# Parts and tables of the second block's head, its last modulations, unread matmuls at the router and another ring of weight homes

## The chip, the cores and the metric

One core of a Trainium2 chip. The metric is the device time of one launch in microseconds (us), taken as the median of several runs. The kernel before the change stands at 1537.5 us (3 runs, 1537.04 to 1538.98).

## The reference, cut to what matters

Two transformer blocks run one after the other over 256 tokens of 1024 features. The first has two layers (a linear-recurrence mixer over latent and context tokens, then a window attention), each with a squared-ReLU MLP. The second is where most of the change lies:

```python
mod = jax.nn.silu(c) @ w_ada + b_ada
sh1, sc1, g1, sh2, sc2, g2 = jnp.split(mod, 6, axis=-1)
h = _rms(x, norm1_g) * (1.0 + sc1) + sh1
z = h @ w_in                      # rq, rf, ri, rg, aq, ak, av, iq, ik, iw
rec = _hgrn2(rq, rf, ri, rg, ...)            # gated recurrence, 4 heads
att = _dsa_attention(aq, ak, av, iq, layernorm(ik), iw, rel_bias)
x = x + g1 * (concat(rec, att) @ w_out)
h2 = _rms(x, norm2_g) * (1.0 + sc2) + sh2
x = x + g2 * _hier_moe(h2, ...)   # 16 experts in 4 groups, 2 of one group per token
```

`_dsa_attention` scores every key with a small indexer (`iq`, `ik`, `iw`), keeps the best, and adds a bias that is looked up in `rel_bias` by bucket of distance. All of it is float32.

## The kernel before, in words

**Products.** A float32 operand is cut in two parts that TensorE (PE) takes: `split` copies it into the rounded high part (on ScalarE, ACT, or VectorE, DVE) and subtracts that from the source for the low part (L251, on DVE or GpSimd, POOL). A product is then three matmuls, high by high, low by high, high by low (`mm_t` L344 to L346, `mm3` L319 to L321). `wload` brings 1 MB of a weight into a tile of the ring `wr` over SyncE's DMA queue (SP), and `wsplit` cuts it into two tiles of `wh` and two of `wl`; `lengs` names the engine that makes each of the two low parts. `rsqrt` is an addition on DVE (L238 or L240) and a power on POOL (L241).

**Order.** A scheduler places the instructions on their engines, by priority in the order in which the program writes them; every engine then runs its own list in order. `tc.issue_after` holds instructions behind a named one. In the attention loop and the expert part PE's and SP's lists are as the program writes them.

**Modulations.** `fill` (L398 in `mods_ev`) makes one block of 512 columns of a modulation vector with matmuls on raw weights (`wr<-w_ada`). 24 such blocks are spread over the program. `mods_col` (L463) transposes a finished one. The last three, of the second block, are (2,9), after the second MLP, and (2,10) and (2,11), at steps u = 10 and 11 of the head loop.

**Head of the second block.** After the MLP, `x2_chain(a)` normalises token tile a: a layer norm (L1349, L1350) and a root mean square. `transpose_tok` (L506) turns it, and `affine_split` scales, shifts and splits it into `hB` (casts L248, subtractions L251). The weights of `w_in` are split by `p_split(n)` for 16 steps, and `p_step(n)` multiplies: steps 0 and 1 are pp[0] (L1454), whose first matmuls need `hB` and the weight's parts. The indexer's key `ik` gets a separate product (`kraw`, L319 to L321 on 72 columns) and a layer norm (L1494 to L1499) after its transposes; then stand `p_step(3)`, the transposes of the recurrence's keys (L1510), and a table: `rel_bias` by bucket (a DMA on ACT's queue, one matmul L1528, a copy L1530, a DMA to DRAM). Then PSUM's pools are opened anew, and the head loop runs u = 0 to 11: `h_decay(u)` (first matmuls L1544, tile c), `p_step(4 + u)`, scores and outputs of the recurrence.

**Attention loop.** `d_scores` (L1735, L1737, L1739), `d_exp` on ACT, transposes (L1758), products with the values (L1772), and between them parts of `w_out` and the rest of the recurrence's output.

**Router and experts.** `x3` is transposed and multiplied with the router's weights (`logits_half`, L1880 and L1886); a chain of small DVE operations picks the experts; a product (L1989 to L1993) counts the tokens of each; `one_hot` builds selection matrices, and `gather(p0, p1)` (L2052) multiplies them with the high and low parts of `x3` (`parts_in`, L1902). Expert pairs are gathered as (0,2), (6,8), (2,6). Each of 8 pairs runs W3 and W1 (L2138), W2 (L2164) and a scatter (L2186). Its weights come in 12 transfers of 1 MB, each into a home: a tile of `wx` (x) or of `wr` (r) in one piece, or a tile of `wh` and one of `wl` (h), or two of the ring `t4` (b) in halves. The first 16 homes are listed in HOMES, all others in a ring of 15, HOMES_ON. SP issues the transfers in program order, so one that waits for its home holds all behind it. Tiles of `t4` also hold the split `x3`.

## Time and profile before

| what | value |
|---|---|
| median of 3 runs | 1537.5 us |
| profiled execution: time | 1539.3 us |
| its span | 1537.5 us |
| mean granted PE clock (1.0 is full) | 0.968 |
| PE busy | 1425.8 us (93%) |
| DVE, ACT, POOL busy | 973.6, 548.0, 265.4 us |
| DMA | 332.96 MB, mean 217 GB/s |

PE is busy nearly throughout, so the page's shares say little: what counts is where PE waits, at which clock it runs (a granted clock of 0.5 is 1.2 GHz, 1.0 is 2.4 GHz), and, in the expert part from 1287 us on, whether the weights' DMA stream keeps up. Times in the trace are from the start of the span.

### The profile page before, as it was taken

How to read it: one execution, taken by the hardware profiler on the slowest of the kernel's cores; microseconds unless marked ns; L12 is line 12 of the kernel's file. 1: busy time of each engine (PE TensorE's matmuls, PEld its weight loads, DVE VectorE, ACT ScalarE, POOL GpSimd, SP SyncE). 2: the span in 40 equal slices, each digit the busy share in tenths (PEclk: the TensorE clock that was granted, in tenths of full speed). 3: DMA queues.
4: the chain of work that ended last, by engine and by line, in shares of the span. 5: the costliest groups of instructions: out<-in, count | busy, mean ns of one | idle time of the engine just before them, and what ended most of it. 6: DMA issues, size and time to landing. Idle time of an engine off the chain costs nothing.

```text
span 1537.5 us, 22176 instructions
## 1 busy us (share of the span) xinstructions
PE 1425.8 (93%) x8651; PEld 1076.4 (70%) x8651; DVE 973.6 (63%) x1662; ACT 548.0 (36%) x921; POOL 265.4 (17%) x263
## 2 busy tenths in 40 slices
PE   5999999999999999989989899987898997999996
PEld 3688787798887878869767889976786675532332
DVE  2343797789999887686895775575688346112212
ACT  2342333244323222324573445545553333301001
POOL 0033204100132210221131310012425220000000
PEclk9998999999999999999999999997999798999999
DMA  8740564446779876625613955555334836699996
GB/s 290 268 168 2 192 247 143 164 133 212 256 263 323 278 236 223 211 72 188 170 70 130 339 185 196 192 177 167 117 110 148 288 132 224 246 408 410 411 410 263
DMA packets 189394, 332.96 MB, mean 217 GB/s; under 512 B 12665, under 2 KB 67553, under 8 KB 189282
## 3 DMA queue, kind: packets, MB, share of 16 engines
q1 hardware_dynamic: 175152, 298.77, 55.9%
q0 software_dynamic: 8640, 27.85, 5.0%
q10 hardware_dynamic: 5490, 4.85, 1.1%
q8 instruction: 70, 1.15, 0.3%
q14 instruction: 42, 0.34, 0.1%
HBM read 320.91 MB, written 10.53 MB: 216 GB/s over the span
## 4 chain that ended last, share of the span: by engine, by line
PE 33%; DMA 8%; DVE 6%; issue 3%; POOL 2%; ACT 2%; SPq 0%; DVEq 0%; POOLq 0%; ACTq 0%
PE g L2138 5%; PE g L321 2%; PE g L320 2%; PE g L319 2%; PE x L2164 2%; DMA wh<-w_in 2%; PE g L344 2%; PE g L346 2%; PE g L345 2%; DMA wr<-w_in 2%; PE x L345 2%; DMA wx<-w_in 2%; PE x L346 2%; PE x L344 2%; DMA wr<-mlp_w_in 2%
## 5 line engine op out<-in xcount | busy, mean ns | idle before, releaser
L251 DVE TENSOR_TENSOR wl<-wr,wh 128x1024 fp32r<-128x1024 f32 (+1 forms) x206 | 255.6, 1254 | 65.9 <-ACT wh L244 63.8
L244 ACT ACTIVATE wh<-wr 128x1024 fp32r<-128x1024 f32 (+1 forms) x226 | 228.9, 1027 | 178.9 <-PE g L346 93.0
L344 PE MATMUL g<-wh,h 128*128 128x512 f32 (+1 forms) x624 | 248.6, 401 | 12.5 <-DVE t L1402 5.9
L319 PE MATMUL g<-h,wh 128*128 128x256 f32 (+1 forms) x768 | 249.8, 327 | 3.7 <-DVE t L1031 2.6
L321 PE MATMUL g<-h,wl 128*128 128x256 f32 (+1 forms) x768 | 248.1, 324 | 5.4 <-DVE wl L251 5.3
L320 PE MATMUL g<-h,wh 128*128 128x256 f32 (+1 forms) x768 | 249.4, 325 | 0.2 <-DVE h L251 0.2
L345 PE MATMUL g<-wl,h 128*128 128x512 f32 (+1 forms) x624 | 246.2, 395 | 2.7 <-DVE wl L251 2.7
L346 PE MATMUL g<-wh,h 128*128 128x512 f32 (+1 forms) x624 | 245.6, 395 | 2.0 <-DVE h L1707 2.0
L427 DVE SCALAR_TENSOR_TENSOR t<-wr,cT,t 128x512 f32<-128x512 f32 x231 | 172.0, 780 | 12.3 <-DMA wr<-w_ada_in 5.8
L319 PEld LDWEIGHTS g<-h,wh 128*128 128x128 f32 x768 | 145.9, 190 | 19.3 <-DVE t L1031 3.0
L321 PEld LDWEIGHTS g<-h,wl 128*128 128x128 f32 x768 | 146.1, 190 | 18.4 <-DVE wl L251 6.6
L320 PEld LDWEIGHTS g<-h,wh 128*128 128x128 f32 x768 | 146.2, 190 | 12.2 <-DVE h L251 0.6
L344 PEld LDWEIGHTS g<-wh,h 128*128 128x128 f32 x624 | 119.9, 193 | 42.4 <-issue 9.9
L345 PEld LDWEIGHTS g<-wl,h 128*128 128x128 f32 x624 | 120.2, 193 | 27.0 <-DVE wl L251 3.5
L346 PEld LDWEIGHTS g<-wh,h 128*128 128x128 f32 x624 | 119.8, 192 | 27.4 <-DVE h L1707 3.0
L244 ACT ACTIVATE t<-t 128x512 f32<-128x512 f32 (+7 forms) x83 | 47.3, 591 | 133.2 <-DVE t L2169 73.1
L244 ACT ACTIVATE h<-e 128x512 fp32r<-128x512 f32 (+1 forms) x64 | 33.6, 524 | 142.7 <-DVE e L962 142.7
L251 POOL TENSOR_TENSOR wl<-wr,wh 128x1024 fp32r<-128x1024 f32 x20 | 50.5, 2525 | 193.1 <-ACT wh L244 179.8
L244 ACT ACTIVATE t<-x 128x128 f32<-128x128 f32 (+3 forms) x78 | 30.7, 464 | 147.5 <-PE x L2145 109.9
L244 ACT ACTIVATE e<-g 128x512 f32<-128x512 f32 (+1 forms) x72 | 35.5, 493 | 94.5 <-PE g L321 84.8
L241 POOL TENSOR_TENSOR sm<-sm,mhalf 128x1 f32<-128x1 f32 (+2 forms) x33 | 33.1, 1004 | 149.4 <-DVE sm L238 109.0
L2138 PE MATMUL g<-wr,t 128*32 128x512 f32 (+1 forms) x248 | 51.3, 611 | 4.8 <-DMA wr<-w_in 4.7
(429 smaller groups left out, 2162.5 us busy)
## 6 DMA issues: line engine op xcount, KB each, us to landing
wr<-mlp_w_in SPq DMA_DIRECT2D x64, 1024.0 KB
wr<-w_mod_in SPq DMA_DIRECT2D x40, 1024.0 KB
wr<-w_in SPq DMA_DIRECT2D x32, 1024.0 KB
t<-w_in SPq DMA_DIRECT2D x52, 512.0 KB
wr<-w_ada_in SPq DMA_DIRECT2D x24, 1024.0 KB
wr<-w_in_in SPq DMA_DIRECT2D x16, 1024.0 KB
wx<-w_in SPq DMA_DIRECT2D x14, 1024.0 KB
wh<-w_in SPq DMA_DIRECT2D x24, 512.0 KB
```

The lines of the kernel that those rows point to most:

```text
L241: return po.tensor_tensor(o, o, mhalf[:, :o.shape[1]], op=OP.pow)
L244: return ac.activation(o, i, fn, **k)
L251: (leng or ve).tensor_sub(lo, src, hi.bitcast(F32))
L319: pe.matmul(ps, ah, bh, start=start, stop=False)
L320: pe.matmul(ps, ah, bl, start=False, stop=False)
L321: pe.matmul(ps, al, bh, start=False, stop=stop)
L344: pe.matmul(ps, ah[:, tsl], w[0][:, cs], start=start, stop=False)
L345: pe.matmul(ps, ah[:, tsl], w[1][:, cs], start=False, stop=False)
L346: pe.matmul(ps, al[:, tsl], w[0][:, cs], start=False, stop=stop)
L427: ve.scalar_tensor_tensor(s_, S["v"][:, k % 4], c_, s_, op0=OP.mult, op1=OP.add)
L2138: pe.matmul(ps[c:c + n, :], xg[p][k][:, c:c + n], w[a][k], start=k == 0, stop=k == 7, skip_group_check=True, tile_position=(0, c))
L2164: pe.matmul(yp[hf][c:c + n, :], hT_[:, m * 128 + c:m * 128 + c + n], w[a][hf][m], start=m == 0, stop=m == 3, skip_group_check=True, tile_p ...
```

## The change

Seven edits, with no arithmetic added to the result:

1. The bias table moves from behind `p_step(3)` into the second MLP (chunk c = 4).
2. Block (2,9) of the modulations is held behind the last DVE operation of `x2_chain(0)`, and its transpose comes after the split of `kraw`.
3. The splits of n = 1 and 2 of `w_in` are held behind the last operation of `transpose_tok` of token tile 0 and 1, and their low parts go to DVE.
4. In pp[0] the order of the three kinds of matmul becomes high by high, low by high, high by low (the low weights last).
5. `p_step(2)` and `p_step(3)` come before the product of `ik` and before its transposes and layer norm.
6. Blocks (2,10) and (2,11) move from the head loop into the first two turns of the attention loop.
7. `keep_on` puts 4, 12 and 8 matmuls (128x128 by 128x512, bf16), whose results nothing reads, behind the last transposes of `x3`, behind the logits and behind the count; HOMES_ON becomes another ring.

```diff
-        (leng or ve).tensor_sub(lo, src, hi.bitcast(F32))
+        return (leng or ve).tensor_sub(lo, src, hi.bitcast(F32))
...
+        if c == 4:
+
+            rb = t1()[:32, :8]
+            ac.dma_start(rb, I["rel_bias_2"])
+            cload_into(t2(), ["buck"])
+            ps = mmps((8, 384))
+            pe.matmul(ps, rb, CT["buck"][:32], start=True, stop=True)
+            tb = t2()[:8, :384]
+            ve.tensor_copy(tb, ps)
+            btab = dp.tile([8, 384], F32, name="btab")
+            po.dma_start(btab, tb)
...
     hB = Opnd(256)
-    x2_chain(0)
-    fill(len(fills) - NF[4], last=True)
-    ve.scalar_tensor_tensor(sB2, vec(2, 4, 0), 1.0, ncol[:, 8:16], op0=OP.add, op1=OP.mult)
-    transpose_tok(xs[0], hB, 0, sB1, bB1)
+    done = x2_chain(0)
+    with tc.issue_after(done.ins):
+        fill(len(fills) - NF[4])
+    hdone = [transpose_tok(xs[0], hB, 0, sB1, bB1)]
     x2_chain(1)
...
-            pw[n] = wsplit(wload(src), lengs=(po, po) if n == 1 else (ve, po))
+            raw = wload(src)
+            if n < 3:
+                late((hdone[n - 1],), lambda: pw.__setitem__(n, wsplit(raw)))
+            else:
+                pw[n] = wsplit(raw, lengs=(ve, po))
...
-        for a, b in ((0, 0), (0, 1), (1, 0)):
+        for a, b in ((0, 0), (1, 0), (0, 1)):
...
     split(kraw_, ikh, ikl)
+    mods_col(*turns.pop())
+    ve.scalar_tensor_tensor(sB2, vec(2, 4, 0), 1.0, ncol[:, 8:16], op0=OP.add, op1=OP.mult)
+    p_step(2)
     ps = xps((72, 256))
...
-    p_step(2)
+    p_step(3)
     ikT = t1()
...
         later.append(turn)
-    p_step(3)
...
-    for f in later:
-        f()
-    later.clear()
-
-
-    rb = t1()[:32, :8]
-    ac.dma_start(rb, I["rel_bias_2"])
-    cload_into(t2(), ["buck"])
     cload_into(t1(), ["anti"])
-    ps = xps((8, 384))
-    pe.matmul(ps, rb, CT["buck"][:32], start=True, stop=True)
-    tb = t2()[:8, :384]
-    ve.tensor_copy(tb, ps)
-    btab = dp.tile([8, 384], F32, name="btab")
-    po.dma_start(btab, tb)
...
         p_step(4 + u)
-        if u >= 10:
-            fill(last=u == 11)
...
-    HOMES, HOMES_ON = "xxbbrrrrrbbbhhhh", "xxbrrrrrbhhhhbb"
+    HOMES, HOMES_ON = "xxbbrrrrrbbbhhhh", "xxbrrrrrhhhhbbb"
...
             d_scores(i + 1)
+        if i < 2:
+            fill()
...
+        if keep:
+            keep_on(keep, a)
...
+    def keep_on(n, after=None):
 
         with ExitStack() as es:
-            for i_ in after:
-                es.enter_context(tc.issue_after(i_.ins))
-            fn()
+            if after is not None:
+                es.enter_context(tc.issue_after(after.ins))
+            ps = mmps()
+            for _ in range(n):
+                a = pe.matmul(ps.rearrange("p (a b) -> p a b", a=4), ltb, onesb[:, None, :].to_broadcast([128, 4, 128]),
+                              start=True, stop=True, skip_group_check=True)
+        return a
...
-        logits_half(0, cb)
+        aftl = logits_half(0, cb, 4 * cb)
+    keep_on(12, aftl)
...
-        pe.matmul(ps[:, 2], onesb, sel[:, t], start=False, stop=t == 1, skip_group_check=True)
+        aftl = pe.matmul(ps[:, 2], onesb, sel[:, t], start=False, stop=t == 1, skip_group_check=True)
+    keep_on(8, aftl)
```

(`late` itself only moves up, unchanged; the other functions gained a return value.)

How the order moves, at three places.

POOL's list in the second block's head, before: `wl` are low parts of weights, `sm` the powers of the norms, `t` the gate's product in `ev_rf`.

```order
L251 TENSOR_TENSOR wl_9363<-wr_9360,wh_9362 128x1024
L241 TENSOR_TENSOR sm_9243<-sm_9243,mhalf 128x1
L251 TENSOR_TENSOR wl_9367<-wr_9360,wh_9366 128x1024
L241 TENSOR_TENSOR sm_9255<-sm_9255,mhalf 128x1
L251 TENSOR_TENSOR wl_9451<-wr_9444,wh_9450 128x1024
L241 TENSOR_TENSOR sm_9334<-sm_9334,mhalf 128x1
L241 TENSOR_TENSOR sm_9346<-sm_9346,mhalf 128x1
L1373 TENSOR_TENSOR t_1612_9461<-t_1612_9461,t_1374_8073 128x512
L1373 TENSOR_TENSOR t_1614_9467<-t_1614_9467,t_1374_8073 128x512
L251 TENSOR_TENSOR wl_9526<-wr_9519,wh_9525 128x1024
L251 TENSOR_TENSOR wl_9619<-wr_9612,wh_9618 128x1024
L241 TENSOR_TENSOR sm_9591<-sm_9591,mhalf 128x1
```

The same stretch after the change:

```order
L241 TENSOR_TENSOR sm_9253<-sm_9253,mhalf 128x1
L241 TENSOR_TENSOR sm_9265<-sm_9265,mhalf 128x1
L241 TENSOR_TENSOR sm_9340<-sm_9340,mhalf 128x1
L241 TENSOR_TENSOR sm_9352<-sm_9352,mhalf 128x1
L1393 TENSOR_TENSOR t_1615_9467<-t_1615_9467,t_1374_8073 128x512
L1393 TENSOR_TENSOR t_1617_9473<-t_1617_9473,t_1374_8073 128x512
L251 TENSOR_TENSOR wl_9509<-wr_9502,wh_9508 128x1024
L251 TENSOR_TENSOR wl_9602<-wr_9595,wh_9601 128x1024
L251 TENSOR_TENSOR wl_9738<-wr_9731,wh_9737 128x1024
L241 TENSOR_TENSOR sm_9667<-sm_9667,mhalf 128x1
```

The four powers of the two token tiles are no longer mixed with three subtractions; the powers of `ik`'s layer norm (the last row, and one more like it) now have three subtractions ahead of them, where two stood before.

PE's list at the end of the head loop and the start of the attention loop, before (`g<-wr,cT` is a block of modulations, L344 to L346 the last `p_step`, L1735 to L1739 scores; the first of the two blocks stands further up, this is the second):

```order
L344 MATMUL g_10542<-wh_10537,h_1563_9236 128x512
L345 MATMUL g_10542<-wl_10538,h_1563_9236 128x512
L346 MATMUL g_10542<-wh_10537,h_1565_9238 128x512
L398 MATMUL g_10653<-wr_10654,cT_105 32x128 x16
L398 MATMUL g_10653<-wr_10672,cT_105 32x128 x16
L1735 MATMUL s_10722<-t_1591_9357,t_1590_9356 128x256
L1737 MATMUL s_10722<-t_1855_10521,t_1666_9710 128x256
```

After the change, from the same matmul of `p_step` on:

```order
L346 MATMUL g_10542<-wh_10537,h_1569_9248 128x512
L1745 MATMUL s_10644<-t_1594_9363,t_1593_9362 128x256
L1747 MATMUL s_10644<-t_1855_10521,t_1666_9710 128x256
L1749 LDWEIGHTS identb
L1749 MATMUL s_10644<-mb_10458,identb 128x256
L1745 MATMUL s_10648<-t_1594_9363,t_1593_9362 128x256
L1747 MATMUL s_10648<-t_1855_10521,t_1666_9710 128x256
L1749 LDWEIGHTS identb
L1749 MATMUL s_10648<-mb_10458,identb 128x256
L398 MATMUL g_10663<-wr_10664,cT_105 32x128
```

The first score of the attention loop follows the last `p_step` at once. Of the first block one matmul stands behind the second score tile (the last row); the rest of it follows the fourth of the 16 score tiles, and the second block the sixth.

SP's list of weight transfers at W2 of the second pair, before:

```order
L1671 DMA t_2091_11717<-w_2_in 128x1024
L1671 DMA t_2092_11718<-w_2_in 128x1024
L1671 DMA wh_11721<-w_2_in 128x1024
L1671 DMA wl_11722<-w_2_in 128x1024
L1671 DMA wh_11725<-w_2_in 128x1024
L1671 DMA wl_11726<-w_2_in 128x1024
```

After the change:

```order
L1681 DMA wh_11744<-w_2_in 128x1024
L1681 DMA wl_11745<-w_2_in 128x1024
L1681 DMA wh_11748<-w_2_in 128x1024
L1681 DMA wl_11749<-w_2_in 128x1024
L1681 DMA wh_11752<-w_2_in 128x1024
L1681 DMA wl_11753<-w_2_in 128x1024
L1681 DMA wh_11756<-w_2_in 128x1024
L1681 DMA wl_11757<-w_2_in 128x1024
L1681 ISA
L1681 DMA t_2103_11765<-w_2_in 128x2x512
L1681 ISA
L1681 DMA t_2104_11766<-w_2_in 128x2x512
```

Four homes of `wh` and `wl` now stand ahead of the pair of `t4` tiles that stood ahead of them.

## Rows read from the trace of the kernel before

**Rows 1.** The chain that ended last, expert part: start us, us, engine, tile.

```profile
1387.29 12.74 DMA wx<-w_in
```

**Rows 2.** Timeline of SP's queue at W2 of the second pair: start us, us.

```profile
1320.72 15.82 SPq L1671 DMA_DIRECT2D t<-w_in  x2
```

**Rows 3.** Windows: us, busy PE, PEld, DVE, ACT, POOL, PE clock, DMA share, GB/s.

```profile
950.00:1028.00 78.00, 78.00 (x481) 70.42 (x480) 48.38 (x60) 39.32 (x54) 0.00 (x0) 1.00 0.62 202
1212.00:1224.00 12.00, 12.00 (x34) 7.60 (x33) 5.06 (x15) 3.48 (x11) 4.13 (x3) 0.50 1.02 389
1278.00:1280.00 2.00, 1.33 (x8) 1.22 (x8) 1.27 (x4) 1.00 (x1) 0.00 (x0) 0.67 1.07 413
1320.00:1340.00 20.00, 20.00 (x94) 11.39 (x92) 5.48 (x10) 8.11 (x11) 0.00 (x0) 1.00 0.35 126
1380.00:1520.00 140.00, 124.89 (x712) 42.37 (x706) 27.95 (x49) 13.08 (x25) 0.00 (x0) 0.99 1.04 411
```

**Rows 4.** Timeline of POOL in the second block's head: start us, us, engine, line.

```profile
1028.38 3.47 POOL L251 TENSOR_TENSOR wl<-wr,wh 128x1024 fp32r<-128x1024 f32 x1 [112.78 <-ACT wh L244]
1031.82 0.56 POOL L241 TENSOR_TENSOR sm<-sm,mhalf 128x1 f32<-128x1 f32 x1
1032.36 2.34 POOL L251 TENSOR_TENSOR wl<-wr,wh 128x1024 fp32r<-128x1024 f32 x1
```

**Rows 5.** Timeline of DVE, same stretch.

```profile
1028.25 0.15 DVE L238 TENSOR_SCALAR sm<-sm 128x1 f32<-128x1 f32 x1
1028.32 1.28 DVE L1349 SCALAR_TENSOR_TENSOR t<-t,sm,t 128x1024 f32<-128x1024 f32 x1
1032.41 3.37 DVE L1350 SCALAR_TENSOR_TENSOR t<-t,sm,t 128x1024 f32<-128x1024 f32 x1 [2.81 <-POOL sm L241]
```

**Rows 6.** Timeline of PE, same stretch.

```profile
1038.36 1.33 PE L506 MATMUL x<-c_ident,t 128*128 128x128 f32 x5 [4.99 <-DVE t L1352]
...
1043.05 2.07 PE L1454 MATMUL g<-h,h 128*128 128x512 f32 x4 [0.63 <-DVE h L248]
```

**Rows 7.** Timeline of PE behind step 3 of the projections.

```profile
1081.27 1.03 PE L1510 MATMUL x<-c_ident,t 128*128 128x128 f32 x8
...
1086.19 0.80 PE L1528 MATMUL x<-t,t 32*8 32x384 f32 x2 [3.34 <-DMA t<-rel_bias_in]
1087.72 0.77 PE L1544 MATMUL c<-h,t 128*128 128x512 f32 x1 [0.73 <-DVE t L1530]
```

**Rows 8.** Timelines of ACT and DVE, same stretch.

```profile
1081.41 1.06 ACT L244 ACTIVATE wh<-wr 128x1024 fp32r<-128x1024 f32 x1 [0.44 <-PE g L320]
...
1081.29 1.11 DVE L1499 TENSOR_SCALAR t<-x,sm 128x64 f32<-128x64 f32 x4 [2.33 <-POOL sm L241]
```

**Rows 9.** Timeline of PE at the start of the attention loop.

```profile
1197.58 1.96 PE L398 MATMUL g<-wr,cT 128*32 128x128 f32 x64
...
1203.95 0.67 PE L1735 MATMUL s<-t,t 64*128 64x256 f32 x2 [0.50 <-DVE md L400]
...
1210.32 1.17 PE L1735 MATMUL s<-t,t 64*128 64x256 f32 x2 [2.01 <-ACT t L244]
```

**Rows 10.** Timeline of PE at the router and in the first pairs.

```profile
1278.02 1.33 PE L1886 MATMUL o<-t,t 128*128 128x20 f32 x8 [0.80 <-ACT t L244]
1283.88 0.21 PE L1989 MATMUL x<-t 128*128 128x32 bf16 x1 [4.53 <-DVE t L1983]
...
1286.95 6.44 PE L2052 MATMUL x<-h,h 128*128 128x256 f32 x32 [2.80 <-DVE h L2019]
...
1307.89 4.10 PE L2052 MATMUL x<-h,h 128*128 128x256 f32 x32
...
1325.66 1.89 PE L2138 MATMUL g<-wl,t 128*64 128x512 f32 x8
...
1329.42 7.42 PE L2052 MATMUL x<-h,h 128*128 128x512 f32 x32
```

**Rows 11.** Timeline of DVE at the router.

```profile
1277.51 1.28 DVE L1902 SCALAR_TENSOR_TENSOR h<-t,rr,h 128x1024 fp32r<-128x1024 f32 x1 [0.52 <-ACT h L244]
```

More of the change, by code (lines that the diff above doesn't have):

```diff
@@ L489, in affine_split @@
         hi, lo = dst.span(k, nk, c0, c0 + n)
-        split(hv, hi, lo, heng=ve)
+        return split(hv, hi, lo, heng=ve)
     def transpose_in(srcs, dst, c0, sc, bi, ks=range(0, 8, 2)):
@@ L506, in transpose_tok @@
                 pe.transpose(ps[:, j], src[:, c128(k + j)], ident)
-            affine_split(ps, dst, k, 4, c0, 128, sc, bi)
+            a = affine_split(ps, dst, k, 4, c0, 128, sc, bi)
+        return a
     W = I["ev_w_in"][0]
@@ L1328, in emit, with late @@
                 mm_t(accp[t, hf], hids[7], c128(t), k, pw[hf][k], False, k == 3)
+    def late(after, fn):
+        with ExitStack() as es:
+            for i_ in after:
+                es.enter_context(tc.issue_after(i_.ins))
+            fn()
     xs = []
@@ L1351, in x2_chain @@
         ss = rms_rows(zz, w_ if a else xsq)
-        ve.tensor_scalar(w_[:, HF[0]], zz[:, HF[0]], ss, None, op0=OP.mult)
+        done = ve.tensor_scalar(w_[:, HF[0]], zz[:, HF[0]], ss, None, op0=OP.mult)
         act(w_[:, HF[1]], zz[:, HF[1]], AF.Copy, scale=ss)
         xs.append(w_)
+        return done
     hB = Opnd(256)
-    x2_chain(0)
-    fill(len(fills) - NF[4], last=True)
-    ve.scalar_tensor_tensor(sB2, vec(2, 4, 0), 1.0, ncol[:, 8:16], op0=OP.add, op1=OP.mult)
-    transpose_tok(xs[0], hB, 0, sB1, bB1)
+    done = x2_chain(0)
+    with tc.issue_after(done.ins):
+        fill(len(fills) - NF[4])
+    hdone = [transpose_tok(xs[0], hB, 0, sB1, bB1)]
     x2_chain(1)
@@ L1450, in emit @@
         if t:
-            transpose_tok(xs[1], hB, 128, sB1, bB1)
-        for a, b in ((0, 0), (0, 1), (1, 0)):
+            hdone.append(transpose_tok(xs[1], hB, 128, sB1, bB1))
+        for a, b in ((0, 0), (1, 0), (0, 1)):
             for k in range(8):
-                pe.matmul(pp[0][t], hB[k][a][:, c128(t)], pw[k // 4][k % 4][b], start=k + a + b == 0, stop=k + a == 8)
+                pe.matmul(pp[0][t], hB[k][a][:, c128(t)], pw[k // 4][k % 4][b], start=k + a + b == 0, stop=k + b == 8)
     p_split(2)
@@ L1873, in x3_add, with logits_half @@
         return ve.tensor_add(x3[t][:, cs], x3[t][:, cs], tmp)
-    def logits_half(t, cb):
+    def logits_half(t, cb, keep=0):
         ps = pst("s", (128, 4, 128))
         for j in range(4):
-            pe.transpose(ps[:, j], x3[t][:, c128(4 * cb + j)], ident)
+            a = pe.transpose(ps[:, j], x3[t][:, c128(4 * cb + j)], ident)
+        if keep:
+            keep_on(keep, a)
         xT = t2(F32, (128, 4, 128))
@@ L1885, in logits_half @@
         for j in range(4):
-            pe.matmul(lps[t], xT[:, j], wgs[:, 4 * cb + j], start=cb + j == 0, stop=cb + j == 4)
+            a = pe.matmul(lps[t], xT[:, j], wgs[:, 4 * cb + j], start=cb + j == 0, stop=cb + j == 4)
+        return a
     def rms_in(t):
@@ L1903, in parts_in @@
         return a
-    def late(after, fn):
+    def keep_on(n, after=None):
         with ExitStack() as es:
-            for i_ in after:
-                es.enter_context(tc.issue_after(i_.ins))
-            fn()
+            if after is not None:
[4 more added lines that the diff above has]
+                              start=True, stop=True, skip_group_check=True)
+        return a
     x3_dram = dp.tile([256, 1024], F32, name="x3_dram")
```

## The prediction

> **What bounds the kernel now.** I read the chain of waits from its end first. In the expert part its last long links are weights, the first of them a wait of 12.74 us that PE ends at 1387.29 [rows 1]. From 1380 to 1520 the DMA share is 1.04 at 411 GB/s while PE is busy 124.89 of 140 us [rows 3]: there the stream of weights sets the end, and PE only follows. The stream began late. SP's queue shows why: two transfers into `t4` tiles, the first W2 home of the second pair, hold the queue for 15.82 us from 1320.72 [rows 2], and in the window 1320 to 1340 the DMA share is 0.35 [rows 3]. Nothing else could be issued past them. PE meanwhile was never idle. So the end is 1336.5 plus a stream at full rate, and 1336.5 is when `gather(2,6)`, which starts at 1329.42 and takes 7.42 us [rows 10], has read the split `x3` that lies in those tiles. Two things can therefore move the end: what brings that gather forward (all the work of PE before it, one for one), and what is let through the queue ahead of it.
>
> Before 1330 I looked for places where PE waits. The head of the second block: 4.99 us before the first transposes and 0.63 before pp[0] [rows 6]; 3.34 and 0.73 us around the bias table [rows 7]. The attention loop's start: 0.50 and 2.01 us, and then score rows that take 1.17 us where they took 0.67 [rows 9], at a granted clock of 0.50, which is 1.2 GHz [rows 3]. The router: waits of 0.80, 4.53 and 2.80 us, and a gather that takes 6.44 us at the low clock where one of the same shape takes 4.10 at the full one [rows 10].
>
> **The change, part by part.**
>
> *Table in the MLP.* The MLP is full on PE (78.00 of 78.00 us [rows 3]), so the table's matmul costs there what it takes: 0.80 us in its row at the low clock [rows 7], half of that at the full clock. Its DMA is issued far ahead on ACT's list, during the first block's attention. **+0.4** (+0.4 to +0.8). Copy and DMA to DRAM lie beside PE's work.
>
> *Splits of n = 1, 2 and the order in pp[0].* The norm's power was ready on DVE at 1028.40 but ran at 1031.82, because POOL was in a low part of 3.47 us [rows 4, 5]. DVE's next step then took 3.37 us beside POOL's second low part, where its twin of the same shape took 1.28 [rows 5]. With POOL free the step begins near 1029.65 (its predecessor's end) and takes 1.28: it ends at 1030.9 in place of 1035.8, 4.85 us earlier, and the transposes go from 1038.36 to about 1033.5. Behind them the order now puts no transpose of the modulation, and the 0.63 us goes too. The low parts move to DVE, each no longer than a step of that size alone (1.28); they now stand in the second tile's chain, and high by low comes last so that PE does not wait for them. **-5.5** at the end of pp[0]. Bounds: -3.4 if only the wait for POOL (1031.82 less 1028.40) goes, -7.0 if the second tile's wait goes as well. The block (2,9) stays hidden in the wait of PE before the transposes.
>
> *Projections before `ik`.* `p_step(3)` now ends before the transposes of `ik`, and the bias table no longer stands between it and the first matmul of `h_decay(0)`. Before, that matmul came 6.45 us after the projections' end (1081.27 to 1087.72 [rows 7]). The new order puts another wait there: tile c waits for the layer norm of `ik`, whose power stands on POOL behind the low part of the next weights, and that waits for ACT's copy, which waits for `p_step(3)`'s last matmuls. From their end: 1.06 (ACT copy [rows 8]) + 2.34 (low part) + 2 x 0.56 (powers [rows 4]) + 0.55 (half of the four scalings' 1.11 [rows 8]) = 5.1 us, with hand-overs some 5.4. **-1.0**. Bounds: 0 if POOL's low part takes 3.47 us as it did beside DVE [rows 4]; -4.9, all of 3.34 + 0.80 + 0.73 [rows 7], if the norm is early.
>
> *Two blocks of modulations.* They leave the path before the loop: 2 x 1.96 and the wait of 0.50 for the last of them [rows 9], -4.4. In the loop they cost 3.9 again at the full clock. Against that, the 2.01 us of waiting go, as ACT's copy of `w_out`, which blocked its exponentials, now stands behind four of them; and the work keeps the clock up for part of the 12 us at 0.50 [rows 3], where each of about ten score rows loses 0.5 us (1.17 against 0.67 [rows 9]), 5 us in all. I count 1.9 of these 5, so that the loop comes out even. **-4.4**. Bounds: -7.5 with all 5 gained, +3.4 with the blocks at half clock (7.8) and nothing given back.
>
> *Unread matmuls.* No row is of 128x512 bf16. The nearest is the gather's 512 columns, 7.42/32 = 0.23 us each at the full clock [rows 10], double at half. Twelve need 2.8 us and stand in a wait of 4.53; eight need 1.9 in one of 2.80: covered. If they hold the clock, the first gather falls from 6.44 to 4.10: -2.3. The logits' last matmuls waited 0.80 for ACT [rows 10], whose copy now precedes the split of `x3`: -0.8. A low part of 1.28 us that lay in a wait of DVE [rows 11] now stands inside its chain: +1.3. **-1.9**. Bounds: -2.7, and +1.9 if the clock falls all the same and the 5.5 and 3.7 us at half clock overrun their waits.
> Before the gap the trace shows PE busy 1.33 of 2 us with transposes and 20-column products, and a clock of 0.67 in that window [rows 3]. [...]
>
> *Ring.* The `t4` pair now stands behind four h homes. Their tiles are read by the first pairs' W1, in four groups of 1.89 us of which the last starts at 1325.66 [rows 10], so they can be filled between about 1322 and 1333, inside the stretch that was at 0.35 [rows 3]. When the gather ends, the stream is four homes further: 4 x 1.049 MB / 411 GB/s [rows 3] = 10.2 us. **-10.2**. Bounds: 0 if the stream stalls again later for as much; -13.3, all the idle DMA time of that window, 20 x (1 - 0.35/1.04).
> The Trainium skill (DMA: Bandwidth & Descriptors, Where 436 GB/s comes from) puts the limit of HBM reads at about 358 GB/s per core. The window shows 411, so the measurement decides; by the page's figure four homes would be 11.7 us.
>
> The sum: +0.4 - 5.5 - 1.0 - 4.4 - 1.9 - 10.2 = -22.6. From the profiled execution's 1539.3 that is 1516.7; that execution lay 1.8 above the median, so the median comes to 1537.5 - 22.6 = **1515**. PE per pair stays below the stream (124.89 of 140 us busy), so the end keeps following the stream.
>
> **The rivals.**
> *The clock falls at the router all the same.* For: it fell while PE was 1.33 of 2 us busy with transposes and small products [rows 3], and only four unread matmuls are put among these; the twelve and the eight would then run at half clock and overrun their waits by 0.7 and 0.9 us, and the gather would stay at 6.44. Against: twelve in a row leave little of the gap idle. That term at +1.9 in place of -1.9: 1519. [...]
> *The ring gives nothing* (the wait only moves). For: the ring holds as many `t4` pairs as before. Against: after the gather those tiles stay free. Without that term: 1537.5 - 12.4 = 1525.
> *The blocks run at half clock in the loop.* For: the loop is at 0.50 in [rows 3], and each wait for ACT invites it. Against: the blocks themselves are work without waits. 7.8 us more in that term: 1523.
> *A stall per round of the ring: slower.* The new ring asks for `t4` pairs as three, then two x, then one: eight tiles within six homes, where the old one asked for six within five. If fewer than eight are free, the third pair waits for experts' reads, in each of the five later rounds, with a stream that has no slack. At 6 us a round (15.82 is what one such wait held SP [rows 2]) that is +30: 1545. It decides from 22.6/5 = 4.5 us a round. Against: by the program's allocations nine tiles are free after `gather(2,6)`.
> *Nothing of it shows:* the head's gain eaten by the new wait on POOL, the clock down at the router, the ring even; about 1536.
>
> **How the numbers follow.** Forecast 0.52, router's clock 0.12, ring 0.14, half clock in the loop 0.12, stalls 0.06, nothing 0.04. The forecast's own range, from the bounds that may well combine, is 1508 to 1522, which holds the router's case too; the next two reach 1528 with their own spread. 1507 to 1528 leaves out the last two and a tail below: 2 in 10. A difference of 0.2% (3 us) is what a measurement of this kernel can tell. Faster by more: 0.90; within: 0.04; slower: 0.06.
>
> **What would show it.** In the changed profile: DVE's second norm step (L1350) at 1.3 us and the transposes near 1033; tile c some 5.4 us after `p_step(3)`, ended by DVE or POOL; scores at 0.67 us through the loop; a clock of 1.0 from 1278 on and a first gather of 4.1 us; no wait of 15 us on SP, a DMA share well above 0.35 in the 20 us before `gather(2,6)` ends, and 1.04 afterwards. I am wrong if the stream shows gaps after that gather, if PE and not the stream ends the expert part, or if the gather is not 12 us earlier than 1329.

## The result and the profile after

| | before | changed |
|---|---|---|
| median of 5 runs (lowest to highest) | 1537.5 us (1535.15 to 1541.18) | 1515.59 us (1514.22 to 1525.65) |
| ratio with its 95% interval | | 0.9873 [0.9839, 0.9906] |
| profiled execution, its span | 1539.3, 1537.5 us | 1525.65, 1523.9 us |
| mean granted PE clock | 0.968 | 0.977 |

The median fell by 21.9 us (19.5 by the ratio); 1515 was forecast. The profiled execution of the changed kernel is the longest of its five. It reached the end of the second MLP 12.6 us later than the profiled execution before (1040.64 against 1028.01, the last statistics of `x2_chain(0)` on DVE). 9.8 of these were already lost at the MLP's first transposes (851.24 against 841.40), ahead of which no edit changes PE's matmuls; two profiles of code that is the same up to there (the kernel before and the ring alone, e2 below) differ by 7.3 us at that point. So I compare stages, from landmark to landmark, and not whole profiles. A second profile of the changed kernel (`e9_changed_control` below) stands beside the first:

| stage | before | changed | changed, e9 |
|---|---|---|---|
| last statistics of x2_chain(0) to the first transposes | 10.35 | 5.92 | 5.92 |
| to the end of p_step(3) | 42.91 | 35.76 | 35.75 |
| to the first matmul of tile c | 6.45 | 6.44 | 6.46 |
| to the first score of the attention loop | 116.23 | 112.42 | 112.96 |
| to the count of tokens | 79.93 | 77.46 | 72.82 |
| to the first gather | 3.07 | 3.17 | 3.18 |
| to gather(2,6) | 42.47 | 40.21 | 41.39 |
| to the last wait for a tile of `wx` | 182.49 | 174.15 | 174.14 |
| to the end | 25.59 | 27.73 | 25.93 |

From those statistics to the end it is 509.5 us before, 483.3 and 478.5 changed. That is 26.2 and 31.0 less, more than any median shows. One profile of the kernel before is a rough yardstick here too: the ring alone (e2) runs the same code up to the experts and takes 493.2, although its ring saves only some 8 of these 16.3 us.

**The head.** DVE's timeline of the changed kernel, where [rows 5] stood:

```profile
1040.64 0.21 DVE L1366 BATCH_NORM_AGGREGATE sm<-sm 128x2 f32<-128x12 f32 x1
1040.89 0.15 DVE L238 TENSOR_SCALAR sm<-sm 128x1 f32<-128x1 f32 x1
1040.96 1.28 DVE L1368 SCALAR_TENSOR_TENSOR t<-t,sm,t 128x1024 f32<-128x1024 f32 x1
1042.69 1.29 DVE L1369 SCALAR_TENSOR_TENSOR t<-t,sm,t 128x1024 f32<-128x1024 f32 x1 [0.46 <-POOL sm L241]
```

The second step takes 1.29 us where it took 3.37, and waits 0.46 for POOL where it waited 2.81. PE's timeline behind it, where [rows 6] and [rows 7] stood:

```profile
1046.56 1.09 PE L506 MATMUL x<-c_ident,t 128*128 128x128 f32 x8 [0.56 <-DVE t L1371]
1049.69 2.08 PE L1478 MATMUL g<-h,h 128*128 128x512 f32 x4 [2.03 <-DVE h L248]
...
1082.45 1.04 PE L1536 MATMUL x<-c_ident,t 128*128 128x128 f32 x8
1088.76 0.77 PE L1556 MATMUL c<-h,t 128*128 128x512 f32 x1 [5.27 <-DVE t L1526]
```

The waits for the bias table (3.34 and 0.73) are gone, and one of 5.27 us for the layer norm of `ik` stands in their place. POOL's timeline says why: the first power stands behind a low part of weights, and the second comes only after the first tile's scaling on DVE.

```profile
1083.60 2.34 POOL L251 TENSOR_TENSOR wl<-wr,wh 128x1024 fp32r<-128x1024 f32 x1 [7.46 <-ACT wh L244]
1085.90 0.55 POOL L241 TENSOR_TENSOR sm<-sm,mhalf 128x1 f32<-128x1 f32 x1
1087.43 0.55 POOL L241 TENSOR_TENSOR sm<-sm,mhalf 128x1 f32<-128x1 f32 x1 [0.99 <-DVE sm L238]
```

The diff takes one more thing out of this stretch, which the list of edits does not name: the two transposes of the normed `ik`, which stood right behind those of the keys (at 1082.14 before), now come in the head loop (at 1097.71).

**The router.** PE's timeline, where [rows 10] stood:

```profile
1270.62 1.03 PE L1927 MATMUL g<-t 128*128 128x512 bf16 x4
...
1272.38 2.75 PE L1927 MATMUL g<-t 128*128 128x512 bf16 x12
1278.64 0.21 PE L2009 MATMUL x<-t 128*128 128x32 bf16 x1 [3.51 <-DVE t L2003]
...
1278.77 3.38 PE L1927 MATMUL g<-t 128*128 128x512 bf16 x8
```

The twelve unread matmuls end in time and leave a wait of 3.51 us; behind it the eight take 3.38, nearly double, so the clock had fallen there after all.

**The stream.** Windows of the kernel before: from 20 us ahead of `gather(2,6)` to its end, and the 43 us that follow (columns as in [rows 3]):

```profile
1309.00:1337.00 28.00, 27.06 (x139) 15.86 (x138) 5.16 (x8) 12.11 (x21) 0.58 (x1) 1.00 0.54 201
1337.00:1380.00 43.00, 41.94 (x308) 14.93 (x311) 7.73 (x18) 4.14 (x8) 0.00 (x0) 1.00 1.03 402
```

The same stretches of the changed kernel, about that gather (1322.02 in place of 1329.42), and the long one of [rows 3]:

```profile
1302.00:1330.00 28.00, 27.06 (x138) 15.73 (x138) 5.32 (x9) 12.24 (x21) 0.58 (x1) 1.00 0.93 345
1330.00:1372.00 42.00, 40.94 (x298) 14.46 (x298) 7.57 (x17) 3.75 (x8) 0.00 (x0) 1.00 1.03 391
...
1380.00:1500.00 120.00, 109.46 (x634) 38.74 (x623) 23.99 (x43) 10.45 (x21) 0.00 (x0) 1.00 1.04 411
```

The stretch before the gather's end went from 0.54 to 0.93. SP's queue shows that the pair of `t4` tiles still waits, but now with four homes sent ahead of it (three further rows lie between those shown):

```profile
1318.44 0.33 SPq L1681 DMA_DIRECT2D wh<-w_in  x1
...
1321.07 0.40 SPq L1681 DMA_DIRECT2D wl<-w_in  x1
1321.68 12.20 SPq L1681 DMA_DIRECT2D t<-w_in  x6
```

In the chain of waits the first long link of weights in the expert part began at 1387.29 before [rows 1]. Now it begins at 1421.79, 34 us later though the gather is 7 us earlier; until then PE bounds this part:

```profile
1421.79 13.28 DMA wr<-w_in
```

The Trainium skill (DMA: Bandwidth & Descriptors, Where 436 GB/s comes from) gives about 358 GB/s as the limit of HBM reads of a core; both kernels hold 411 for 120 us and more, so here the measurement decides.

### The profile page after: what moved, and what is told of

It reads as the page before. It is cut to its first block, busy times and chain, and to the rows that moved or that the text cites. A ratio compares the mean times of both kernels' runs of the same rounds, so it can differ in the third digit from the quotient of the medians.

```text
span 1523.9 us, 22219 instructions
## 1 busy us (share of the span) xinstructions
PE 1418.7 (93%) x8675; PEld 1069.9 (70%) x8675; DVE 971.2 (64%) x1665; ACT 548.5 (36%) x921; POOL 255.3 (17%) x260
## 3 DMA queue, kind: packets, MB, share of 16 engines
q10 hardware_dynamic: 5490, 4.85, 1.1%
## 4 chain that ended last, share of the span: by engine, by line
PE 36%; DVE 6%; DMA 5%; issue 2%; POOL 2%; ACT 2%; DVEq 0%; POOLq 0%; ACTq 0%; SPq 0%
PE g L2159 6%; PE x L2185 3%; PE g L321 3%; PE g L319 3%; PE g L320 3%; PE g L344 2%; DMA wr<-w_in 2%; PE x L344 2%; PE x L345 2%; PE x L346 2%; PE g L346 2%; PE g L345 2%; DMA wr<-mlp_w_in 2%; ACT t L244 1%; PE g L2207 1%
## 5 line engine op out<-in xcount | busy, mean ns | idle before, releaser
L251 DVE TENSOR_TENSOR wl<-wr,wh 128x1024 fp32r<-128x1024 f32 (+1 forms) x209 | 259.3, 1255 | 64.1 <-ACT wh L244 62.2
L344 PE MATMUL g<-wh,h 128*128 128x512 f32 (+1 forms) x624 | 247.8, 400 | 12.5 <-DVE t L1422 7.3
L346 PE MATMUL g<-wh,h 128*128 128x512 f32 (+1 forms) x624 | 243.8, 392 | 2.0 <-DVE h L1717 2.0
L344 PEld LDWEIGHTS g<-wh,h 128*128 128x128 f32 x624 | 119.1, 191 | 42.2 <-issue 10.3
L346 PEld LDWEIGHTS g<-wh,h 128*128 128x128 f32 x624 | 119.0, 191 | 27.5 <-DVE h L1717 3.0
L244 ACT ACTIVATE t<-g 128x512 f32<-128x512 f32 (+1 forms) x68 | 34.7, 520 | 55.8 <-PE g L346 26.1
L2159 PE MATMUL g<-wr,t 128*32 128x512 f32 (+1 forms) x248 | 48.8, 595 | 4.6 <-DMA wr<-w_in 4.5
```

What stands on the lines that cost most here:

```text
L244: return ac.activation(o, i, fn, **k)
L251: return (leng or ve).tensor_sub(lo, src, hi.bitcast(F32))
L344: pe.matmul(ps, ah[:, tsl], w[0][:, cs], start=start, stop=False)
L346: pe.matmul(ps, al[:, tsl], w[0][:, cs], start=False, stop=stop)
L2159: pe.matmul(ps[c:c + n, :], xg[p][k][:, c:c + n], w[a][k], start=k == 0, stop=k == 7, skip_group_check=True, tile_position=(0, c))
```

## The experiments

The theory was close to that of the forecast: the ring gives some 8 to 10 us, the head 5 to 10, the blocks 4 to 7 and the unread matmuls about 2, all adding up, while the table gives nothing. Against it stood that one part alone does it, or that the loop's clock is luck. Ratios are to runs of the kernel before on the same chip, in three sessions: its median was 1542.73 us for e1 to e4, 1539.22 for e5 to e8 and 1543.92 for e9 to e11. An interval is some 4 us to either side.

**The changed kernel again**, without an edit.

> The changed kernel once more, nothing edited: a second profile, since its first profiled execution took 1525.65 us, 10 above its own median, and lost 12.6 us before the second block, where no instruction was moved. If that loss is a matter of the single execution, the second MLP's last statistics (1028.01 in the profile of before, 1040.64 in the changed one) come within 4 us of 1028 here, and the time is 1514 to 1518. If the change itself costs something in the first block, they stay near 1040. In both cases the second block, from those statistics to the end, is 483 us as in the first profile (509.5 before), give or take 1.5.

1519.08 us, ratio 0.9844 [0.9818, 0.9870]: 23.7 us faster. The second block takes 482.6 us, as expected, but the time is 1 us above its range and the statistics come at 1039.34: by the rule set beforehand that speaks for a cost of the change in the first block. Over all profiles it stays open. The MLP's first transposes come at 841.40, 848.66 and 849.31 us in the three kernels with the table at its old place (before, e2, e7) and at 846.13 to 852.59 in the ten with it in the MLP. One instruction of the change does stand ahead of them: the table's DMA on ACT's queue, at 758.9 to 765.8 us. PE's waits for DVE at the attention's transposes (L1175 in before and e2, L1176 in the others) sum to 5.3 to 6.6 us in the three and 6.7 to 8.5 in the ten. A cost of one or two us there isn't excluded, and was not tried by itself.

**The ring alone**, in the kernel before.

```diff
-    HOMES, HOMES_ON = "xxbbrrrrrbbbhhhh", "xxbrrrrrbhhhhbb"
+    HOMES, HOMES_ON = "xxbbrrrrrbbbhhhh", "xxbrrrrrhhhhbbb"
```

> The kernel before with the new ring of homes alone. My sum said 10.2 us less: about 1527. The changed kernel's profile shows only 6.2 less from the start of gather(2,6) to the end (201.88 against 208.08), as 8.3 of stream, with a last product that ran at half clock for 2; by that the ring alone is worth 6 to 8: 1529.5 to 1531.5. If the wait only moves, 1537.

1532.06 us, ratio 0.9940 [0.9918, 0.9961]: 10.7 us faster by the medians, 9.3 by the ratio, both more than the 6 to 8 expected. From `gather(2,6)` to the last wait for `wx` it takes 174.48 us (182.49 before). In the window from 1320 the share that was 0.35 is

```profile
1320.00:1340.00 20.00, 20.00 (x94) 11.39 (x92) 5.48 (x10) 8.10 (x11) 0.00 (x0) 1.00 0.91 335
```

**The ring undone**, in the changed kernel (the same line the other way).

> The changed kernel with the old ring. If the ring's gain is of its own, this is 6 to 8 us slower than the changed kernel (1522 to 1524), with SP's wait of some 15 us before gather(2,6) ends back again. If the earlier gather alone would have done it (the stream then starts 20 us earlier), the times differ by less than 3.

1529.74 us, ratio 0.9926 [0.9910, 0.9942]: 10.7 us slower than e1. The stretch is back at 182.30, and SP's timeline has the old wait again, 15.84 us where [rows 2] had 15.82:

```profile
1305.15 15.84 SPq L1681 DMA_DIRECT2D t<-w_in  x2
1321.05 0.42 SPq L1681 DMA_DIRECT2D wh<-w_in  x1
```

Alone and undone agree: the ring's gain does not depend on the other edits.

**The splits of n = 1 and 2 undone**: at their old place and on POOL.

```diff
-            if n < 3:
-                late((hdone[n - 1],), lambda: pw.__setitem__(n, wsplit(raw)))
-            else:
-                pw[n] = wsplit(raw, lengs=(ve, po))
+            pw[n] = wsplit(raw, lengs=(po, po) if n == 1 else (ve, po))
```

> The changed kernel with the low parts of n = 1 and 2 back on GpSimd and not held behind the casts; all else as changed. In my sum this was the part worth 5.5 us at the end of the projections. The changed profile showed 11.6 there, of which about 5 are clock: 1054 to 1062 and 1071 to 1076 were at 0.5 to 0.7 before and at 1.0 in the changed kernel. If the wait for GpSimd causes both, step 3 of the projections ends 10 to 11 us later than in the changed kernel, measured from the MLP's last statistics (52 against 41.7), and the time is 1524 to 1527. If the clock comes from the order of pp[0] or of the steps, it ends 5 to 6 later: 1520 to 1522.

1527.84 us, ratio 0.9900 [0.9883, 0.9916]: 8.8 us slower than e1. The first transposes come 10.36 us after the statistics, as before, and DVE's long step is back:

```profile
1045.17 3.38 DVE L1369 SCALAR_TENSOR_TENSOR t<-t,sm,t 128x1024 f32<-128x1024 f32 x1 [2.81 <-POOL sm L241]
```

`p_step(3)` ends 47.93 us after the statistics, against 41.67 in e9 (43.10 in e1) and 53.26 before (50.64 in e2, whose code is the same there). So the splits carry 4.8 to 6.3 us of this stretch. What is left to the kernel before, 2.7 to 5.3 us, comes with the other edits of the head (the order in pp[0], the block (2,9), the order of the steps) or with the clock; no run parts these. Part of it all is clock: the first transposes and pp[0] now stand behind waits of 5.00 and 3.32 us, and pp[0] begins at half clock, as windows of e4 show:

```profile
1051.00:1058.00 7.00, 3.55 (x12) 2.79 (x13) 6.97 (x13) 3.21 (x9) 2.29 (x1) 0.50 1.07 396
1058.00:1063.00 5.00, 5.00 (x16) 3.97 (x15) 3.32 (x6) 1.15 (x2) 1.52 (x1) 0.61 0.82 236
```

The kernel before ran at half clock in pp[0] too; these are the products of its second token tile:

```profile
1054.00:1058.00 4.00, 3.60 (x11) 3.14 (x12) 2.07 (x4) 2.73 (x6) 0.00 (x0) 0.50 0.41 131
1058.00:1062.00 4.00, 4.00 (x14) 3.17 (x14) 1.12 (x2) 1.29 (x2) 1.27 (x1) 0.72 0.02 5
```

In the changed kernel the first four products of pp[0] are still slow (2.08 us from 1049.69, as the 2.07 in [rows 6]); behind them its first profile runs from 1054 to 1076 at 1.00, e1 at 0.84.

**The unread matmuls undone**: the three calls of `keep_on` are left out.

```diff
-        if keep:
-            keep_on(keep, a)
...
-    keep_on(12, aftl)
...
-    keep_on(8, aftl)
```

> The changed kernel without the 24 unread matmuls (4, 12 and 8). By my term they give 1.9 us, 2.3 of them in the first gather (6.44 to 4.10). In the three profiles with them the router's way from the first gather to gather(2,6) took 40.2, 41.5 and 41.4 us, against 42.5 and 41.9 without. If the clock's hold is theirs, the first gather here takes 6.4 us again, and the time is 1 to 2 us above the changed kernel. If they only burn time, the gather is as fast as with them, and the time is equal or up to 1 less.

1521.26 us, ratio 0.9869 [0.9837, 0.9901]. Against 0.9844 and 0.9841 (e1, e9) that is some 4 us slower, but the intervals overlap. PE's timeline has a wait of 6.11 us, one of 2.89, and the gather at the low clock:

```profile
1272.97 0.21 PE L2006 MATMUL x<-t 128*128 128x32 bf16 x1 [6.11 <-DVE t L2000]
...
1276.14 6.74 PE L2069 MATMUL x<-h,h 128*128 128x256 f32 x32 [2.89 <-DVE h L2036]
```

The three profiles without unread matmuls have this gather at 6.44, 5.80 and 6.74 us; the ten with them have it between 4.10 and 5.45, mean 4.7: 1.6 us less. The ten fall into two groups, 5.34 to 5.45 in e1, e3, e4 and e9 and 4.10 to 4.37 in the others. The first four took 72.7 to 73.0 us through the loop ahead, as e5 did (72.73), the others 74.2 to 77.5. Beside its like, e5 loses 1.3 to 1.4 us in the gather. One run shows the eight at full pace: e6, where DVE makes the first low part of `x3` (1.28 us) ahead of its chain and not inside it, and the wait that is left is 1.93:

```profile
1276.45 0.19 PE L2009 MATMUL x<-t 128*128 128x32 bf16 x1 [1.93 <-DVE t L2003]
...
1276.57 1.89 PE L1927 MATMUL g<-t 128*128 128x512 bf16 x8
1279.54 4.10 PE L2073 MATMUL x<-h,h 128*128 128x256 f32 x32 [1.08 <-DVE h L2040]
```

**The two blocks undone**: back in the head loop.

```diff
-        if i < 2:
-            fill()
...
+        if u >= 10:
+            fill(last=u == 11)
```

> The changed kernel with the two blocks of modulations back at steps u = 10 and 11. By my term (4.4 before the loop, nothing in it) it is 4.4 us slower. The profiles put the way from tile c to the first score at 116.2 without and 112.4 to 115.1 with the move, and the loop from there to the count at 79.9 and 74.3 without, 77.5, 72.7, 72.8 and 73.0 with it. So by the profiles: 3 to 5 slower in all, if the loop keeps its clock either way. If the blocks in the loop cost their full 3.9, the times are equal.

1522.95 us, ratio 0.9888 [0.9850, 0.9927]: by the ratios some 7 us slower than e1 and e9, though the intervals overlap here too. The way to the first score is 3.7 us longer than in e9 (116.68 against 112.96) and the loop to the count 3.4 us (76.17 against 72.82); the gather, at the full clock in e6, gives some of this back, so that from tile c to `gather(2,6)` e6 is 5.7 us longer (236.06 against 230.35). Two windows of e6, the loop's start and the 12 us behind it:

```profile
1200.00:1209.00 9.00, 7.13 (x25) 4.07 (x26) 3.91 (x8) 4.24 (x10) 1.94 (x2) 0.88 0.96 343
1209.00:1221.00 12.00, 12.00 (x32) 7.30 (x32) 6.20 (x18) 3.77 (x12) 3.04 (x3) 0.50 1.04 393
```

The same two of e9, which has the blocks in the loop:

```profile
1195.00:1204.00 9.00, 8.66 (x90) 5.29 (x90) 3.81 (x12) 3.56 (x12) 1.03 (x1) 1.00 0.50 126
1204.00:1216.00 12.00, 11.96 (x122) 8.59 (x120) 7.40 (x22) 7.95 (x21) 4.71 (x4) 1.00 0.82 303
```

At half clock PE is never idle (12.00 of 12.00), and yet it does less. The clock fell here in all three profiles without the blocks in the loop (before, e2, e6), at a price that varies: 79.93, 74.26 and 76.17 us to the count. Of the ten with them it is 1.00 in nine through the first 27 us of the loop; in the first profile of the changed kernel it fell all the same, from 1203 on, and that is the 77.46 of the table above. There is a second pattern in these rows: the nine have a clock of 0.83 to 0.87 in the 10 us ahead of the first score, the other four 1.00. The dip comes at the one place or at the other, and ahead of the loop it is cheap (112.96 us in e9 against 112.42). So the edit moved the dip in most executions; that the blocks' work alone holds the clock isn't shown.

**The table undone**: behind the keys' transposes again, the new order of the steps kept (code as in the removed lines of the change).

> The changed kernel with the bias table back behind the transposes of the keys. My theory now: the table's move gained nothing at tile c, since the layer norm's powers behind GpSimd's low part end there at the same 6.44 us as the DMA did, and it costs about 2 us in the MLP (from the last MLP's transposes to its statistics 188.2 to 189.4 with it, 186.6 without). Then this kernel is equal to the changed one or up to 2 us faster: -2 in the MLP, and 0 to +1.5 at tile c, where the DMA's wait and the norm's run side by side. If my forecast's step was right (1.0 gained at tile c, 0.4 lost), it is 0.6 slower or more.

1519.00 us, ratio 0.9849 [0.9816, 0.9882], no different from e1 and e9. From `p_step(3)` to tile c it takes 6.90 us, of which these waits on PE:

```profile
1081.94 1.43 PE L1538 MATMUL g<-t,t 32*8 32x384 f32 x2 [2.27 <-DMA t<-rel_bias_in]
1085.40 0.76 PE L1554 MATMUL c<-h,t 128*128 128x512 f32 x1 [2.03 <-DVE t L1540]
```

The table hides in the time that the norm of `ik` takes anyway: moving it gained 0.5 us there (6.90 against 6.44), and its matmuls take 0.81 in the MLP.

**The norm of `ik` between the halves of `p_step(3)`**, with one power for both tiles; the split of n = 5 is held behind its last operation.

```diff
+            for m in range(2):
+                if m and mid:
+                    mid()
...
+            if n == 5:
+                late((hdone[2],), lambda: pw.__setitem__(n, wsplit(raw, lengs=(ve, po))))
...
+        rsqrt(mv[:, :, 1], mv[:, :, 1], 1e-6)
...
+    p_step(3, ik_norm)
```

> A version that may beat both: the changed kernel with the transposes and the layer norm of ik between the two halves of step 3 of the projections, with one power for both tiles, and the split of n = 5 held behind it. If the wait before tile c is the powers behind GpSimd's low part, tile c starts 2.4 to 3 us after the projections' end in place of 6.44, and the time falls by 3 to 4. If something else ends there next (the evacuation of the keys, the opening of PSUM), the wait stays above 5.

1515.91 us, ratio 0.9849 [0.9812, 0.9887]. Tile c comes 2.89 us after `p_step(3)` (6.46 in e9), but `p_step(3)` ends 2.3 us later: the products of `ik` now wait 1.99 us for their low parts, and the clock is 0.66 in the 4 us behind that. No gain that can be told.

**The parts of `ik`'s weights early, too**: e8, with the load ahead of `x2_chain(0)` and the split behind the first tile's transposes. e9 is the changed kernel beside it.

```diff
+    kraw_ = t4(F32, (128, 8, 72))
+    sy.dma_start(kraw_, kview(I["w_in_2"][0], 0, 8, 4096, 72))
     done = x2_chain(0)
...
+    late((hdone[0],), lambda: split(kraw_, ikh, ikl))
```

> The changed kernel unedited, beside the two versions below on the same chip, since the first block alone differs by up to 12 us between profiled executions: what beats it has to beat it here. 1515 to 1520, and 483 us from the MLP's last statistics to the end, give or take 3. If the attention loop keeps its clock, as in all but one profile with the blocks in it, the way from the first score to the count is 72.7.

> The version with the norm between the halves of step 3, and on top of it the parts of ik's weights loaded before the norm of the first token tile and split beside the second tile's. In the run of that version PE still waited 1.99 us for the low part of these weights and the clock fell to 0.66 behind it, so that the projections ended 2.3 later than in the changed kernel. If that wait brought the clock down, the projections end 40 to 41 us after the MLP's statistics, tile c starts at 43 to 44 (48.1 in the changed kernel), and the time is 4 to 5 below the changed one. If another wait takes its place, tile c stays at 46 or later.

e9: 1518.93 us, ratio 0.9841 [0.9807, 0.9875]; its second block takes 478.5 us, 1.5 below the range expected. e10: 1516.25 us, ratio 0.9826 [0.9793, 0.9859]. The wait for the low parts is gone and `p_step(3)` ends 1.5 us earlier, but tile c waits again, now for DVE:

```profile
1084.30 0.76 PE L1567 MATMUL c<-h,t 128*128 128x512 f32 x1 [4.65 <-DVE t L1404]
```

Of that DVE operation (the gate's evacuation) its timeline says that a low part of weights stood ahead of it:

```profile
1080.47 1.10 DVE L1534 TENSOR_SCALAR t<-x,sm 128x64 f32<-128x64 f32 x4 [0.82 <-POOL sm L241]
1081.48 2.34 DVE L251 TENSOR_TENSOR wl<-wr,wh 128x1024 fp32r<-128x1024 f32 x1
1083.75 0.41 DVE L1404 TENSOR_TENSOR t<-g,t 128x256 f32<-128x256 f32 x1
```

Tile c is 2.2 us nearer to the statistics than in e9 (45.90 against 48.13 us). But in this profile the MLP ahead took 190.39 us (187.67 in e9), so that from the MLP's first transposes to tile c it is 0.5 us longer than e9. The median is the lower of the pair, but the intervals overlap: I don't call it faster.

**Eight unread matmuls ahead of the last W2**, on top of e10. In the first profile of the changed kernel 16 products there ran at half clock (5.35 us, behind a wait of 2.32), which made its end 27.73 us long.

```diff
     tr7, w = (turn(he), scatter_in(7)), W2.pop(7)
+    keep_on(8)
```

> The same with 8 more unread matmuls behind the last transposes of the last pair, where PE waits 2.32 us for ACT and the next products then run at 1.2 GHz (5.35 us for 16 in five of the profiles, 3.65 in others). If the wait brings the clock down, these products take 3.65 and the time is 1.7 below the previous version. If the clock falls for what came before (the waits for the weights' DMA), the 8 run at half clock, take 3.4 us, and it is 1 us slower.

1517.28 us, ratio 0.9827 [0.9792, 0.9862]: no gain. The wait fell to 0.59 us and those products ran at the full clock. They did so in e10 as well, without the eight and behind the wait of 2.32 us, so this doesn't show that the eight held it. In both the clock fell one group earlier, behind a wait for the last weights (2.53 us in e10, 2.26 in e11), and the end is 27.74 us long (27.57 in e10):

```profile
1494.16 0.64 PE L2196 MATMUL x<-wx,t 128*64 128x512 f32 x1 [2.26 <-DMA wx<-w_in]
...
1496.22 1.06 PE L2196 MATMUL x<-wx,t 128*64 128x512 f32 x1
...
1502.63 0.64 PE L2196 MATMUL x<-wx,t 128*64 128x512 f32 x1 [0.59 <-ACT t L244]
1503.11 0.59 PE L2196 MATMUL x<-wx,t 128*64 128x512 f32 x1
```

## Why the prediction was right

The forecast was right as a whole and in its two largest mechanisms, the ring and the splits: -22.6 us, against -21.9, -23.7 and -25.0 in the three sessions with the changed kernel. That the sum came so near is partly luck: the ring gave some 2 less than its term, the unread matmuls little or nothing net and tile c nothing, while the blocks gave 1 to 3 more and the head up to `p_step(3)` 2 to 6 more than forecast. Step by step:

| term | forecast (bounds) | between landmarks | by undoing it |
|---|---|---|---|
| table in the MLP | +0.4 (to +0.8) | +0.1 to +1.9 against e7, +1.1 to +2.8 against before | none to be told (e7) |
| splits, order in pp[0] | -5.5 (-3.4 to -7.0) | -5.6 to -9.0 at the end of pp[0]; splits alone -4.8 to -6.3 | -8.8 (e4) |
| p_step(3) first, tile c | -1.0 (0 to -4.9) | 0.0 at tile c; -1.1 to -3.4 in steps 1 to 3 | not tried |
| two blocks | -4.4 (-7.5 to +3.4) | -3.7 and -3.4 | about -7 (e6) |
| unread matmuls | -1.9 (-2.7 to +1.9) | -1.3 to -2.6 against e5; -0.9 to +0.4 against before | about -4, unclear (e5) |
| ring | -10.2 (0 to -13.3) | -6.7 to -8.5, mean -7.9 | -10.7 (e2 and e3) |

What was undone sums to more than the whole (some 30 us); each difference of two medians carries 4 us or more, so only the ring and the splits stand by their times alone, and the others by their landmarks.

*Splits.* Right: the transposes came 4.43 us earlier (4.85 forecast), and DVE's step took 1.29. Wrong in a detail: the wait ahead of pp[0] did not go but grew from 0.63 to 2.03 us; pp[0] still began 6.0 us earlier. Missed: half clock in the second tile's products (0.61 from 1054 to 1062 before, 1.00 from 1058 to 1066 in the changed kernel's first profile) stood in no term. pp[0] ended 26.40 us after the statistics (28.62 in e1), against 35.38 before and 34.25 in e2; in e4, with the new order and without the splits, 32.76.

*Table and tile c.* The term of -1.0 failed. I counted one serial pass over POOL, 5.4 us; it took 6.44. The two powers do not follow each other, since the second tile's statistics stand behind the first tile's scaling on DVE (1085.90 and 1087.43). The place was right, the chain was one turn longer. The gain that the trace shows is ahead of tile c, from the end of pp[0] to that of `p_step(3)`: 14.5 us in e1 and 15.3 in e9 and the first profile, against 16.4 in e2 and 17.9 before. I didn't undo the order of the steps by itself, so how much of it is that order and how much the clock's chance (0.71 from 1071 to 1076 before, 1.00 changed) stays open. In the MLP the stretch from its first transposes to the last statistics was 186.6 us before and in e2, and 187.7 to 189.4 in the changed kernel's three profiles, but also 187.5 in e7 without the table; the table's matmuls take 0.81.

*Blocks.* The mechanism fits the traces (the waits among the first scores are gone, and the clock is up in nine profiles of ten), the size was cautious: I counted 1.9 of the 5 us that the clock could give back, and more came: 3.4 to the count in e6, on top of the 3.7 before the loop, of which the router gives back 1.4. Where the clock fell in spite of it, 62 of the first block's matmuls took 3.64 us in place of 1.95: the third rival is real, and was seen in one profile of ten.

*Unread matmuls.* Half right. The twelve were covered and kept their pace (2.75 us; 2.8 forecast from the gather's columns). They did not hold the clock through the 3.5 us of waiting that were left, and so the eight ran at half clock, wholly or for the most part, in all profiles that have them but e6, and overran their wait by 0.1 us. The gather fell to a mean of 4.7, not 4.10. The +1.3 came as forecast (from the last logits' products to the count 7.16 us, 5.86 before), but not with the unread matmuls: e5 has it (7.17) without them, and e6 (5.59) has them without it. The -0.8 did not come: the four fill that wait and don't shorten it (the last products start 1.01 us after the last transpose, 0.99 in e5 without the four). Net of all that, from the last logits' products to `gather(2,6)` it takes 50.5 to 51.8 us in the changed kernel and its variants (52.6 in e8, 48.8 in e6), 51.4 before and 53.1 in e5: the matmuls pay for the longer chain, and little more. (By the prediction's own row, twelve at half clock would overrun the 4.53 us by 1.0, not 0.7.) The router's rival was right for the eight, and wrong for the twelve and for most of the gather. The Trainium skill (TensorE: Matmul & The Clock Gate, Part 4: PE-mode transpose) has transposes not count as busy in the same way. No run here shows that apart. The window that the prediction reads as transposes and small products holds no transpose: from 1278 to 1280 PE ran eight 20-column products [rows 10], and the window from 1276 to 1278, where the last transposes stand among such products, is at 1.00. So that row does not bear on the rule. Behind the idle 3.51 us the clock fell without a transpose near.

*Ring.* Right in kind; 6.7 to 8.5 us between the landmarks (173.97 to 175.56 us in the eleven profiles with the new ring, 182.49 and 182.30 with the old), where four homes at 411 GB/s are 10.2. Up to the gather's end the stream did gain that: 28 x (0.93 - 0.54) / 1.04 = 10.5 us. About 1.1 are given back in the next 42 us (391 against 402 GB/s); I can't place the rest. No round of the ring stalled: 411 GB/s from 1380 to 1500. The rivals of a ring that gives nothing and of one that stalls are refuted by e2 and e3.

*The signs.* The prediction called itself wrong if the gather did not come 12 us earlier than 1329. In the first profile it came 7.4 earlier (1322.02), since that execution reached the second block 12.6 us later; from the statistics on it came 20.0 earlier, and in e9 it came at 1312.73. No wait of 15 us on SP was to be left: one of 12.20 is, with four homes sent ahead of it. The clock of 1.0 from 1278 on did not hold.

## What to carry to other kernels

Where a DMA queue is served in order, look for the one transfer that waits for its buffer and see which transfers behind it could already go: reordering them gave a stream at its limit some 8 us without touching the stream. A wait of a few us on TensorE can cost twice, once as itself and once as half clock behind it (3.32 us, then 0.50, in e4). Work that must be done anyway was the better filler here (in nine of ten profiles the loop kept its clock), and twelve unread matmuls in front of a gap of 3.51 us that stayed open did not hold the clock, where one of 1.93 left it up. A chain over three engines that replaces a wait is to be counted turn by turn, and kernels with such a clock are compared by landmarks and medians, not by two profiles.

## What the runs showed of the hardware

- The stretch up to the second MLP's first transposes, in which no edit changes PE's matmuls, took 841.4 to 852.6 us over the 13 profiles. That is half of the whole gain, most of it from one execution to the next (841.40 and 848.66 for the same code); its cause stays open.
- The same wait of 2.32 us on PE, for ACT ahead of the last W2, left the clock up in the kernel before (0.59 us for each product behind it) and was followed by its fall in the first profile of the changed kernel (1.06 us). The wait alone doesn't decide: behind it the clock stayed up in six of twelve profiles and fell in six. In e10 and e11 it fell at the wait before, of 2.53 and 2.26 us; in e7 that wait was 2.50 and left it up.
- DVE's L1350 (L1369 after the change; 128x1024, float32), beside a low part on POOL, takes 3.37 and 3.38 us (before, e4); the same operation takes 1.29 with POOL free, in the changed kernel. Before, it ended 1.08 us after POOL's (1035.78 against 1034.70).
